# Retention values of two head pairs in products of 512 columns, weights passing four accumulating banks; keys, queries and the gated unit's operands by halves

## The chip, the cores and the metric

The kernel runs on one core of one Trainium2 chip. The metric is the time of one execution on the device in microseconds (us); less is better. A core has a matrix engine (TensorE, PE in the profile; its weight loads are listed as PEld), a vector engine (VectorE, DVE), an activation engine (ScalarE, ACT), a general engine (GpSimd, POOL), and a queue from which this kernel issues its DMA transfers (SyncE, SP). Each engine works through its own instructions in a fixed order and waits on the others by semaphores.

## The reference

Input and output are 1024 tokens of 1024 channels. There are two layers, each `x = x + mixer(rmsnorm(x))`, and a final rmsnorm. Layer 0 is one input projection that feeds a state-space branch with a gated unit and a retention branch, and an output projection over both. Layer 1 is a convolution module. The change lies in layer 0:

```python
def mixer_ab(h, w_in, ...):
    proj = h @ w_in
    u_s5, g_s5, q, k, v, g_ret = jnp.split(proj, cuts, axis=-1)
    y_s5 = s5_mixer(u_s5, ...)       # ends with y = gelu(y); y * sigmoid(y @ glu_w + glu_b)
    y_s5 = y_s5 * jax.nn.silu(g_s5)
    q, k: (B, L, 8 heads, 64);  v: (B, L, 8 heads, 128)
    y_ret = retention(q, k, v) * jax.nn.silu(g_ret)
    return jnp.concatenate([y_s5, y_ret], axis=-1) @ w_out

def retention(q, k, v):              # chunks of 64 frames
    q = rope(q, positions) * (RET_DK ** -0.5)
    k = rope(k, positions)
    scores = jnp.einsum('bnihd,bnjhd->bnhij', qc, kc) * intra
    intra_out = jnp.einsum('bnhij,bnjhe->bnihe', scores, vc)
    kv = jnp.einsum('bnjhd,jh,bnjhe->bnhde', kc, k_dec, vc)
    # s <- chunk_decay * s + kv, from chunk to chunk
    cross = jnp.einsum('bnihd,ih,bnhde->bnihe', qc, q_dec, s_prev)
    out = intra_out + cross
    return (out - mean) * rsqrt(var + EPS)      # per head
```

## The kernel before

**Products.** A product of two fp32 operands is made of three: each operand is split into a high part (a rounded copy, tile names with h) and a low part (what is left, names with l), and high x high, high x low and low x high are summed in one PSUM bank (`mm3`, L119; 128 contraction rows each, eight row blocks `KB`). Weights arrive as tiles of 128 x 1024 through `wnext` and `wload_pieces` (L87 to L117): a DMA of 512 KB into `wf`, a cast on ACT into `wh` (L115), a subtraction on POOL into `wl` (L116). Each of the three has three buffers, and loads run two tiles ahead of use, in the order that `plan` (L63) writes down. Activations `xs[h]` lie in SBUF, split, in two halves h of 512 tokens.

**Banks.** PSUM has three banks in `ps_mm` (`bank(..., aux=False)`) and five in `ps_aux` in this part of the program.

**Retention** (L766) works on four pairs of heads. `ret_proj(pair)` (L791) projects the keys, then the queries: two halves of 24 products with 512 columns each, the weights stationary, and an eviction on DVE that multiplies by the norm's factor (L804). `turn` (L807) does the rotary positions: four DMAs on SP copy `raw` into `swp` with its blocks of 32 partitions exchanged (L813, one swap buffer), POOL multiplies both by tables (L816, L817; four instructions of half the tokens each), and DVE adds the halves into `krot` or `qrot` (L818). The adds of the keys are held back behind the last query eviction (L824). Then come the values of the pair (L829 to L844): for each of eight token blocks 24 products of 256 columns, here with the tokens as the stationary operand and the weights as the moving one, in a bank of `ps_mm`, and an eviction on ACT (L844).

`y_pass` (L757) belongs to the other branch: it loads outputs of the state-space part, transposed, applies gelu on ACT and stores them on SP; from pair 1 on it is held behind the last statistics of the pair before.

`ret_heads(pair, K, Q, V)` (L847) takes the rotated tiles: eight transposes of the keys (`ktp`, L856), `kt` with the decay on DVE (L858), 28 products `kv` (L870), the states `S` by a chain of DVE instructions (L878, L880), the scores `sp` (L886) and their mask on DVE (`sc`, L892), the outputs `ro` (L912, L917), the per-head norm on DVE (L926, L927, L932, tiles `on` with three buffers), and transposes `rt` of the normalised tiles (L940), multiplied by the gate `grl` (L943) and stored (L946). The two halves of tokens are `0` and `1` in names such as `rt1`. The transposes of a pair come in the order first half head 1, head 0, then second half head 1, head 0, and `on` of the last tile takes a buffer that a transpose of the first half frees.

**Order of the work.** The scheduler of the language merges what is written one after the other: while the heads of one pair wait on DVE, the keys and queries of the next pair run on PE, and PE's order is fixed when the program is built. `chained` (L357) keeps groups of products together, and `issue_after` holds an instruction behind another.

**Changeover.** `layer0_back_and_layer1` (L953) begins with the gated unit. Its operands `y` are loaded by `load_split` (L963) as eight tiles of 128 x 1024 in the weights' `wf` buffers, each split into halves: `yh` on ACT (L950) and `yl` on DVE (L951). The loop at L991 then makes 16 groups of 24 products `mm_glu`. The scheduler runs the first of them beside the heads of pair 3. The table of the convolution, `convw`, is loaded and halved on DVE at L1082 to L1084.

Of the kernel before, what the change touches and what calls it, by code (L numbers as in the profile page):

```python
# [39 lines left out]
class Trunk:  # L40
# [22 lines left out]
    def plan(self):  # L63

        A = self.A
        seq = [(A["w_ab"][nb], f"u{nb}") for nb in range(8)]
        seq += [(A["w_ab"][nb], f"g{nb}") for nb in range(8, 24)]
        for p in range(4):
            seq += [(A["w_ab"][28 + p], f"k{p}"), (A["w_ab"][24 + p], f"q{p}")]
            seq += [(A["w_v"][2 * p + i], f"v{p}_{i}") for i in range(2)]  # L70
        seq += [(A["w_glu"][nb], f"glu{nb}") for nb in range(8)]

        def wo(h):
            return [q for nb in range(8) for q in ((A["w_out"][nb], f"wos{nb}_{h}"),
                                                   (A["w_out"][8 + nb], f"wor{nb}_{h}"))]
# [681 lines left out]
    def y_pass(self, rp, cb):  # L757
# [4 lines left out]
        yn = rp.tile([P, P, 8], F32, name=f"yn_{cb}", tag="ynt", bufs=2)  # L762
# [3 lines left out]
    def retention(self, st):  # L766
# [11 lines left out]
        nc.sync.dma_start(self.g128[:], A["ret_g128"])  # L778
        for pair in range(4):
            cur = self.ret_proj(pair)  # L780
# [8 lines left out]
            self.ret_heads(pair, *cur)  # L789

    def ret_proj(self, pair):  # L791
# [5 lines left out]
        def project(nm):  # L797
            w = self.wnext(f"{nm}{pair}")
            raw = raws[nm] = self.rq.tile([P, T], F32, name=f"{nm}raw_{pair}", tag="raw", bufs=2)
            for h in range(2):  # L800
                c = slice(h * HALF, (h + 1) * HALF)
                ps = self.bank(f"mm_{nm}{pair}_{h}", aux=False)
                self.gemm(ps[:], w, self.xs[h])
                last = nc.vector.tensor_tensor(raw[:, c], ps[:], self.R[:, c], op=ALU.mult)  # L804
# [16 lines left out]
        project("k")  # L821
        krot, adds = turn("k")
        last = project("q")
# [4 lines left out]
        for add in adds:  # L828
            add()  # L829

        wv = [self.wnext(f"v{pair}_{i}") for i in range(2)]
        vt = rp.tile([P, 8, 256], F32, name=f"v_{pair}", tag="v", bufs=2)
        for b in range(8):
            ps = self.bank(f"mm_v{pair}_{b}", aux=False)
            h, o = b // 4, (b % 4) * P
            for kb in range(KB):
                xh, xl = self.xs[h][kb]
                i, k4 = kb // 4, kb % 4
                wh = wv[i][0][:].rearrange("p (k a) n -> p k (a n)", a=2)[:, k4, :]
                wl = wv[i][1][:].rearrange("p (k a) n -> p k (a n)", a=2)[:, k4, :]  # L840
                nc.tensor.matmul(ps[:, :256], xh[:, o:o + P], wh, start=kb == 0, stop=False)  # L841
                nc.tensor.matmul(ps[:, :256], xh[:, o:o + P], wl, start=False, stop=False)  # L842
                nc.tensor.matmul(ps[:, :256], xl[:, o:o + P], wh, start=False, stop=kb == KB - 1)  # L843
            nc.scalar.mul(vt[:, b, :], ps[:, :256], self.Rtok[:, b:b + 1])  # L844
        return krot, qrot, vt

    def ret_heads(self, pair, K, Q, V):  # L847
        nc, rp = self.nc, self.rp
        v = nc.vector

# [11 lines left out]
        for hf in range(2):  # L862
            ps = self.bank(f"kv{hf}_{pair}")
            for b4 in range(4):
# [3 lines left out]
                for hh in range(2):  # L868
                    r = slice(64 * hh, 64 * hh + 64)
                    nc.tensor.matmul(ps[r, b4 * P:(b4 + 1) * P], kt[:, b, r], V[:, b, hh * P:(hh + 1) * P],  # L870
# [32 lines left out]
        for hf in range(2):  # L903
            pss = [self.bank(f"ro{hf}_{2 * pair + hh}") for hh in range(2)]

            def products():
# [7 lines left out]
                for hh in range(2):  # L914
                    for b4 in range(4):
                        b = 4 * hf + b4
                        yield nc.tensor.matmul(pss[hh][:, b4 * P:(b4 + 1) * P], sc[hh][:, b, :],  # L917
                                               V[:, b, hh * P:(hh + 1) * P], start=False, stop=b4 == 3)
# [34 lines left out]
    def layer0_back_and_layer1(self, st):  # L953
# [9 lines left out]
        def load_split(src, name, halves):  # L963
# [6 lines left out]
            if halves:  # L970
                for h in range(2):
                    for kb in range(KB):
# [18 lines left out]
        for nb, h in [(nb, h) for nb in range(6) for h in range(2)] + [(6, 0), (7, 0), (6, 1), (7, 1)]:  # L991
# [14 lines left out]
            v.scalar_tensor_tensor(b[:], sg[:], 0.5, a[:].bitcast(F32), op0=ALU.mult, op1=ALU.subtract)  # L1006
# [77 lines left out]
        v.tensor_scalar(cw[:], cw[:], 0.5, None, op0=ALU.mult)  # L1084
# [261 lines left out]
def layout(inp):  # L1346
# [10 lines left out]
    wv = w[:, 3072:4096].reshape(2, 4, P, 4, 256)  # L1357
# [50 lines left out]
```

## Time and profile before

| | us |
|---|---|
| median of 3 runs | 1220.06 (1220.02 to 1220.82) |
| the profiled execution | 1225.77 |
| its span, first to last instruction | 1224.0 |
| PE busy in it | 1203.9 |
| retention in the trace | about 337 to 556 |
| changeover to the gated unit | about 556 to 594 |

The mean granted clock of PE in the profiled execution is 0.995 of full speed. Busy times of PE are sums of the durations of overlapping products, cut where they overlap, so a busy PE can still be a PE at less than its best pace; the distance between the starts of two products is the measure of pace. Rows that begin with a line such as L841 are groups of instructions: line, engine, operation, tiles (output<-inputs), shape, count, then busy us and mean ns of one, then the idle time of the engine before them and what ended it. Rows that begin with two times are single instructions or short runs of them in order of time.

### The profile page before, as it was taken

The numbers are of one execution on the slowest core, as the hardware profiler recorded it, in microseconds if no ns is written. First come the engines' busy times: TensorE is split into PE (matmuls) and PEld (weight loads), VectorE is DVE, ScalarE is ACT, GpSimd is POOL, SyncE is SP. The second block draws the span as 40 slices with busy tenths as digits, with TensorE's granted clock in tenths as the row PEclk, the third lists the DMA queues.
The fourth block names the chain that finished last, engine by engine and source line by source line (L and its number), as shares of the span: only waits on it lengthen the run. The fifth ranks groups of instructions, "written<-read, shape, count | busy, mean of one in ns | idle before, by whom it ended". The sixth has DMA issues, their size and how long they took to land.

```text
span 1224.0 us, 17472 instructions
## 1 busy us (share of the span) xinstructions
PE 1203.9 (98%) x6676; PEld 1015.3 (83%) x6676; DVE 770.8 (63%) x1357; ACT 470.3 (38%) x698; POOL 719.6 (59%) x472
## 2 busy tenths in 40 slices
PE   9999999999999999998999999999999999999987
PEld 7888888888889999897888787888888887888877
DVE  7965555555414644646646102399999999899664
ACT  7212333232222323234435322554435474435653
POOL 2059988888124333352444553777795789769742
PEclk9999999999999999999999999999999999999998
DMA  9342433333384536376445654533445323345443
GB/s 330 104 138 75 151 126 126 137 123 123 115 258 138 171 106 185 92 215 220 164 155 182 213 167 119 153 103 93 132 147 192 101 69 112 109 124 172 155 147 138
DMA packets 86115, 179.93 MB, mean 147 GB/s; under 512 B 7696, under 2 KB 36624, under 8 KB 85392
## 3 DMA queue, kind: packets, MB, share of 16 engines
q1 hardware_dynamic: 86032, 178.82, 46.2%
q8 instruction: 52, 0.85, 0.3%
q14 instruction: 31, 0.25, 0.1%
HBM read 135.87 MB, written 38.73 MB: 143 GB/s over the span
## 4 chain that ended last, share of the span: by engine, by line
PE 89%; DMA 4%; DVE 2%; ACT 2%; issue 1%; POOL 1%; SPq 1%; DVEq 0%; POOLq 0%; ACTq 0%
PE mm_g L126 7%; PE mm_g L125 7%; PE mm_g L124 7%; PE mm_wo L126 4%; PE mm_wo L125 4%; PE mm_wo L124 4%; PE mm_a L126 2%; PE mm_b L126 2%; PE mm_b L125 2%; PE mm_b L124 2%; PE mm_a L125 2%; PE mm_a L124 2%; PE mm_u L126 2%; PE mm_u L125 2%; PE mm_u L124 2%; PE mm_glu L126 2%
## 5 line engine op out<-in xcount | busy, mean ns | idle before, releaser
L1114 DVE SCALAR_TENSOR_TENSOR cv<-u,convw,cv 128x512 f32<-128x512 f32 x416 | 283.6, 749 | 15.4 <-ACT cv L1106 13.8
L126 PE MATMUL mm_g<-xh,wl_g 128*128 128x512 f32 x256 | 100.8, 394 | 0.0
L125 PE MATMUL mm_g<-xl,wh_g 128*128 128x512 f32 x256 | 100.7, 393 | 0.0
L124 PE MATMUL mm_g<-xh,wh_g 128*128 128x512 f32 x256 | 100.5, 393 | 0.0
L841 PE MATMUL mm_v<-wh_v,xh 128*128 128x256 f32 x256 | 72.5, 283 | 0.6 <-ACT v L844 0.6
L843 PE MATMUL mm_v<-wh_v,xl 128*128 128x256 f32 x256 | 72.5, 283 | 0.0
L842 PE MATMUL mm_v<-wl_v,xh 128*128 128x256 f32 x256 | 72.4, 283 | 0.0
L116 POOL TENSOR_TENSOR wl_v<-wf_v,wh_v 128x1024 fp32r<-128x1024 f32 x8 | 19.6, 2449 | 87.7 <-ACT wh_v L115 87.7
L1102 POOL TENSOR_TENSOR tp<-tp,tp 128x512 f32<-128x512 f32 x48 | 62.2, 1297 | 6.7 <-ACT tp L1101 4.2
L307 DVE TENSOR_TENSOR gt<-mm_g,R 128x512 f32<-128x512 f32 x32 | 21.9, 684 | 59.9 <-PE mm_g L126 59.9
L126 PE MATMUL mm_oc<-zh,wl_woc 128*128 128x512 f32 (+1 forms) x152 | 54.3, 360 | 3.4 <-DVE wl_woc L116 3.4
L125 PEld LDWEIGHTS mm_g<-xl,wh_g 128*128 128x128 f32 x256 | 48.1, 188 | 11.3 <-issue 1.6
L116 POOL TENSOR_TENSOR wl_wos<-wf_wos,wh_wos 128x1024 fp32r<-128x1024 f32 x16 | 38.8, 2426 | 30.9 <-ACT wh_wos L115 30.9
L126 PEld LDWEIGHTS mm_g<-xh,wl_g 128*128 128x128 f32 x256 | 48.0, 188 | 10.6
L1026 DVE TENSOR_TENSOR x<-mm_wo,xr 128x512 f32<-128x512 f32 x16 | 11.1, 691 | 72.1 <-PE mm_wo L126 69.0
L124 PEld LDWEIGHTS mm_g<-xh,wh_g 128*128 128x128 f32 x256 | 48.1, 188 | 9.6
L124 PE MATMUL mm_oc<-zh,wh_woc 128*128 128x512 f32 (+1 forms) x152 | 55.8, 371 | 0.0
L116 POOL TENSOR_TENSOR wl_cb<-wf_cb,wh_cb 128x1024 fp32r<-128x1024 f32 x16 | 38.5, 2408 | 28.0 <-ACT wh_cb L115 23.1
L125 PE MATMUL mm_oc<-zl,wh_woc 128*128 128x512 f32 (+1 forms) x152 | 54.7, 361 | 0.0
L125 PE MATMUL mm_glu<-yl,wh_glu 128*128 128x512 f32 x128 | 50.3, 393 | 2.2 <-DVE yl L951 2.2
L116 POOL TENSOR_TENSOR wl_wor<-wf_wor,wh_wor 128x1024 fp32r<-128x1024 f32 x16 | 38.8, 2426 | 22.7 <-ACT wh_wor L115 22.7
L125 PE MATMUL mm_u<-xl,wh_u 128*128 128x512 f32 x128 | 50.1, 391 | 1.0 <-DVE xl L239 1.0
(384 smaller groups left out, 3728.4 us busy)
## 6 DMA issues: line engine op xcount, KB each, us to landing
wf_g<-w_ab SPq DMA_DIRECT2D x16, 512.0 KB, 4.4
wf_wos<-w_out SPq DMA_DIRECT2D x16, 512.0 KB, 3.7
wf_wor<-w_out SPq DMA_DIRECT2D x16, 512.0 KB, 3.7
wf_cb<-w_c SPq DMA_DIRECT2D x16, 512.0 KB, 3.6
wf_ca<-w_c SPq DMA_DIRECT2D x16, 512.0 KB, 3.7
wf_woc<-w_out_c SPq DMA_DIRECT2D x16, 512.0 KB, 4.0
wf_cg<-w_c SPq DMA_DIRECT2D x11, 512.0 KB, 3.7
u_d<-ut SPq DMA_DIRECT2D x8, 512.0 KB, 3.3
```

The lines of the kernel that those rows point to most:

```text
L116: lo[i].tensor_tensor(wl[:].rearrange(fl)[:, c], wf[:, c], h.bitcast(F32), op=ALU.subtract)
L124: nc.tensor.matmul(ps, wh[:, kb, :], xh, start=start, stop=False)
L125: nc.tensor.matmul(ps, wh[:, kb, :], xl, start=False, stop=False)
L126: self.last_mm = nc.tensor.matmul(ps, wl[:, kb, :], xh, start=False, stop=stop)
L307: nc.vector.tensor_tensor(gt[:, c], ps[:], self.R[:, c], op=ALU.mult)
L841: nc.tensor.matmul(ps[:, :256], xh[:, o:o + P], wh, start=kb == 0, stop=False)
L842: nc.tensor.matmul(ps[:, :256], xh[:, o:o + P], wl, start=False, stop=False)
L843: nc.tensor.matmul(ps[:, :256], xl[:, o:o + P], wh, start=False, stop=kb == KB - 1)
L1026: v.tensor_tensor(t[:], ps[:], xt[:], op=ALU.add)
L1102: gp.tensor_tensor(s0[:], s0[:], sk[:], op=ALU.add)
L1114: v.scalar_tensor_tensor(dst[:], us[i][:, k:k + HALF], cw[:, nb, k:k + 1], accs_[i][:], op0=ALU.mult, op1=ALU.add)
```

## The change

Four things are altered.

1. **Values.** `ret_values(pair)` replaces the values in `ret_proj` and is called for pairs 0 and 2 only. It makes the values of two pairs at once: for each half of the tokens four banks of `ps_aux` are opened, four weight tiles pass, and each weight tile gives every bank 2 x 3 products of 512 columns. A half ends with four evictions of 128 x 512. Each weight tile is loaded once per half, 16 loads of values in all where there were 8. The weights are laid out anew on the host for it.
2. **Order of keys and queries.** `ret_proj` is a generator that stops after the key products. Pair 2's keys are projected ahead of the heads of pair 1; the values of pairs 2 and 3 then come between the heads of pair 1 and those of pair 2. Pair 3's halves come in the order key, query, key, query. There are two swap buffers for one, and one `ynt` buffer for two.
3. **Operands of the gated unit.** `load_split` loads them by halves of the tokens, first all of the first half; a `wf` buffer holds two of them.
4. **The convolution's table** is halved behind the last instruction of the gated unit.

```diff
@@ plan
-            seq += [(A["w_v"][2 * p + i], f"v{p}_{i}") for i in range(2)]
+            if p % 2 == 0:
+                seq += [(A["w_v"][2 * p + j], f"v{p}_{h}_{j}") for h in range(2) for j in range(4)]
@@ y_pass
-        yn = rp.tile([P, P, 8], F32, name=f"yn_{cb}", tag="ynt", bufs=2)
+        yn = rp.tile([P, P, 8], F32, name=f"yn_{cb}", tag="ynt", bufs=1)
@@ retention
+        ahead = None
         for pair in range(4):
-            cur = self.ret_proj(pair)
+            proj = ahead or self.ret_proj(pair)
+            K, Q = list(proj)[-1]
+
+            ahead = pair == 1 and self.ret_proj(pair + 1)
+            if ahead:
+                next(ahead)
+            if pair % 2 == 0:
+                V = self.ret_values(pair)
...
-            self.ret_heads(pair, *cur)
+            self.ret_heads(pair, K, Q, V)
@@ ret_proj
             for h in range(2):
-                c = slice(h * HALF, (h + 1) * HALF)
-                ps = self.bank(f"mm_{nm}{pair}_{h}", aux=False)
-                self.gemm(ps[:], w, self.xs[h])
-                last = nc.vector.tensor_tensor(raw[:, c], ps[:], self.R[:, c], op=ALU.mult)
-            return last
+                yield half(nm, w, raw, h)
...
-            swp = self.rq.tile([P, T], F32, name=f"{nm}swp_{pair}", tag="swp", bufs=1)
+            swp = self.rq.tile([P, T], F32, name=f"{nm}swp_{pair}", tag="swp", bufs=2)
...
-        project("k")
+        k, q = project("k"), project("q")
+
+        for step in ((k, q, k) if pair == 3 else (k, k)):
+            next(step)
+        yield None
         krot, adds = turn("k")
-        last = project("q")
+        for last in q:
+            pass
...
-        wv = [self.wnext(f"v{pair}_{i}") for i in range(2)]
-        vt = rp.tile([P, 8, 256], F32, name=f"v_{pair}", tag="v", bufs=2)
-        for b in range(8):
-            ps = self.bank(f"mm_v{pair}_{b}", aux=False)
...
-                nc.tensor.matmul(ps[:, :256], xh[:, o:o + P], wh, start=kb == 0, stop=False)
-                nc.tensor.matmul(ps[:, :256], xh[:, o:o + P], wl, start=False, stop=False)
-                nc.tensor.matmul(ps[:, :256], xl[:, o:o + P], wh, start=False, stop=kb == KB - 1)
-            nc.scalar.mul(vt[:, b, :], ps[:, :256], self.Rtok[:, b:b + 1])
-        return krot, qrot, vt
+        yield krot, qrot
+
+    def ret_values(self, pair):
+
+        nc = self.nc
+        res = []
+        for h in range(2):
+            vt = self.rp.tile([P, 4, HALF], F32, name=f"v_{pair}_{h}", tag="v", bufs=2)
+            pss = [self.bank(f"mm_v{pair}_{h}_{b}") for b in range(4)]
+            for j in range(4):
+                wh, wl = (t[:].rearrange("p (k a) n -> p k (a n)", a=4) for t in self.wnext(f"v{pair}_{h}_{j}"))
+                for b in range(4):
+                    o = slice(b * P, (b + 1) * P)
+                    for k in range(2):
+                        kb = 2 * j + k
+                        xh, xl = self.xs[h][kb]
+                        nc.tensor.matmul(pss[b][:], xh[:, o], wh[:, k, :], start=kb == 0, stop=False)
+                        nc.tensor.matmul(pss[b][:], xh[:, o], wl[:, k, :], start=False, stop=False)
+                        nc.tensor.matmul(pss[b][:], xl[:, o], wh[:, k, :], start=False, stop=kb == KB - 1)
+            for b in range(4):
+                nc.scalar.mul(vt[:, b, :], pss[b][:], self.Rtok[:, 4 * h + b:4 * h + b + 1])
+            res.append(vt)
+        return res
@@ load_split
-            if halves:
-                for h in range(2):
-                    for kb in range(KB):
-                        f = lp.tile([P, HALF], F32, name=f"{name}f{kb}_{h}", tag="tp", bufs=3)
-                        nc.sync.dma_start(f[:], src[rows(kb), hs(h)])
-                        put(kb, h, f[:])
-            else:
+            for h in range(2):
                 for kb in range(KB):
-                    f = self.wp.tile([P, T], F32, name=f"{name}f{kb}", tag="wf", bufs=3)
-                    nc.sync.dma_start(f[:], src[rows(kb)])
-                    for h in range(2):
-                        put(kb, h, f[:, hs(h)])
+                    if halves:
+                        f = lp.tile([P, HALF], F32, name=f"{name}f{kb}_{h}", tag="tp", bufs=3)[:]
+                        nc.sync.dma_start(f, src[rows(kb), hs(h)])
+                    else:
+
+                        if kb % 2 == 0:
+                            f2 = self.wp.tile([P, 2, HALF], F32, name=f"{name}f{kb}_{h}", tag="wf", bufs=3)
+                        f = f2[:, kb % 2, :]
+                        nc.sync.dma_start(f, src[rows(kb), hs(h)])
+                    put(kb, h, f)
@@ gated unit, convolution
-            v.scalar_tensor_tensor(b[:], sg[:], 0.5, a[:].bitcast(F32), op0=ALU.mult, op1=ALU.subtract)
+            glu_end = v.scalar_tensor_tensor(b[:], sg[:], 0.5, a[:].bitcast(F32), op0=ALU.mult, op1=ALU.subtract)
...
-        v.tensor_scalar(cw[:], cw[:], 0.5, None, op0=ALU.mult)
+        with self.tc.issue_after(glu_end.ins):
+            v.tensor_scalar(cw[:], cw[:], 0.5, None, op0=ALU.mult)
```

In the built program after the change, PE's order between pair 1's last query product and the values of pair 2 is: 48 key products of pair 2, 8 transposes `ktp` of pair 1, 22 query products of pair 2, `kv` of pair 1, scores with 9 query products among them, `ro` of pair 1, the last 17 query products of pair 2, then the 16 transposes `rt` of pair 1 with nothing between them. On DVE, both halves of pair 1's `qrot` and one key eviction of pair 2 come before pair 1's `kt`, and the last normalised tile of pair 1 comes behind pair 2's last query eviction, both halves of its `krot` and two gate products. On SP, pair 1's query swap copies stand behind one gate load for two before.

More of the change, by code (lines that the diff above doesn't have):

```diff
@@ L800, in project, with half @@
             for h in range(2):
-                c = slice(h * HALF, (h + 1) * HALF)
-                ps = self.bank(f"mm_{nm}{pair}_{h}", aux=False)
-                self.gemm(ps[:], w, self.xs[h])
-                last = nc.vector.tensor_tensor(raw[:, c], ps[:], self.R[:, c], op=ALU.mult)
-            return last
+                yield half(nm, w, raw, h)
+        def half(nm, w, raw, h):
+            c = slice(h * HALF, (h + 1) * HALF)
+            ps = self.bank(f"mm_{nm}{pair}_{h}", aux=False)
+            self.gemm(ps[:], w, self.xs[h])
+            return nc.vector.tensor_tensor(raw[:, c], ps[:], self.R[:, c], op=ALU.mult)
         def turn(nm, behind=None):
             raw, tab = raws[nm], tabs[nm]
-            swp = self.rq.tile([P, T], F32, name=f"{nm}swp_{pair}", tag="swp", bufs=1)
+            swp = self.rq.tile([P, T], F32, name=f"{nm}swp_{pair}", tag="swp", bufs=2)
             o = rp.tile([P, T], F32, name=f"{nm}rot_{pair}", tag=f"{nm}rot", bufs=1)
@@ L849, in ret_heads @@
         v = nc.vector
+        val = lambda b, hh: V[b // 4][:, b % 4, (2 * (pair % 2) + hh) * P:(2 * (pair % 2) + hh + 1) * P]
         kt = rp.tile([P, 8, P], F32, name=f"kt_{pair}", tag="kt", bufs=1)
@@ L869, in ret_heads @@
                     r = slice(64 * hh, 64 * hh + 64)
-                    nc.tensor.matmul(ps[r, b4 * P:(b4 + 1) * P], kt[:, b, r], V[:, b, hh * P:(hh + 1) * P],
+                    nc.tensor.matmul(ps[r, b4 * P:(b4 + 1) * P], kt[:, b, r], val(b, hh),
                                      start=True, stop=True)
@@ L917, in products @@
                         yield nc.tensor.matmul(pss[hh][:, b4 * P:(b4 + 1) * P], sc[hh][:, b, :],
-                                               V[:, b, hh * P:(hh + 1) * P], start=False, stop=b4 == 3)
+                                               val(b, hh), start=False, stop=b4 == 3)
             last_ro = self.chained(products())
@@ L1356, in layout @@
     A["w_ab"] = _blocks(order)
-    wv = w[:, 3072:4096].reshape(2, 4, P, 4, 256)
+    wv = w[:, 3072:4096].reshape(4, 2, P, 2, HALF)
     A["w_v"] = wv.transpose(3, 0, 2, 1, 4).reshape(8, P, KB, P)
```

6 lines of the change are left out of this document (removed).

## The prediction

> **What bounds the kernel now.** I read the shares first, then the chain of waits, then a table of stretches, then single instructions.
>
> ```profile
> span 1224.0 us, 17472 instructions
> PE 1203.9 (98%) x6676; PEld 1015.3 (83%) x6676; DVE 770.8 (63%) x1357; ACT 470.3 (38%) x698; POOL 719.6 (59%) x472
> PE 89%; DMA 4%; DVE 2%; ACT 2%; issue 1%; POOL 1%; SPq 1%; DVEq 0%; POOLq 0%; ACTq 0%
> 337.00:556.00 219.00, 218.44 (x1593) 198.53 (x1590) 100.08 (x241) 61.46 (x79) 80.67 (x49) 1.00 0.55 166
> ```
>
> The last row is the retention stage: length, then PE, PEld, DVE, ACT and POOL busy (instructions), granted clock, DMA share, GB/s. Rows of the timeline further down begin with start and duration in us; a bracket gives the idle time before and what ended it. PE has 0.56 us free in 219 us. So only two things count: how long PE needs for its products, and which new wait reaches it. Outside this stage and the changeover to the gated unit (556 to about 594 us) the order of every engine's instructions stays as it is.
>
> **Term 1: the value products.** 768 products of 256 columns become 384 of 512. They overlap in the pipeline, so the price is the distance between two starts, not the duration.
>
> ```profile
> L841 PE MATMUL mm_v<-wh_v,xh 128*128 128x256 f32 x256 | 72.5, 283 | 0.6 <-ACT v L844 0.6
> ...
> 533.11 0.28 PE L841 MATMUL mm_v<-wh_v,xh 128*128 128x256 f32 x1
> ...
> 556.02 0.28 PE L843 MATMUL mm_v<-wh_v,xl 128*128 128x256 f32 x1
> ...
> 356.84 0.39 PE L125 MATMUL mm_q<-xl,wh_q 128*128 128x512 f32 x1
> ...
> 359.10 0.39 PE L126 MATMUL mm_q<-xh,wl_q 128*128 128x512 f32 x1
> ```
>
> Pair 3's 192 value products start over 533.11 to 556.02: 22.91/191 = 0.120 us each. The query products of 512 columns take (359.10-356.84)/10 = 0.226; elsewhere, just after transposes, up to 0.230. I take 0.228: 768 x 0.120 - 384 x 0.228 = 92.2 - 87.6 = -4.6 us (-5.4 to -3.9). A reader of the durations 0.283 and 0.39 would expect -67; that is the trap of this change.
>
> The only PE gap in the stage goes too. It came when an eviction stood behind a gelu on ACT:
>
> ```profile
> 368.68 0.39 PE L841 MATMUL mm_v<-wh_v,xh 128*128 128x256 f32 x1 [0.56 <-ACT v L844]
> ```
>
> Now the next half's first bank is finished 18 products (4.1 us) before it is wanted again, which covers a delay of this size: -0.6 (0 if the gelu falls later in the four). The evictions themselves, 16 wide ones for 32, lie beside PE and count nothing.
>
> **Term 2: weights of pair 0's values.** Each weight tile is now loaded once per half: 16 subtractions on POOL for 8, and a tile lasts 24 x 0.228 = 5.5 us on PE. Query products end at 359.33, so the fourth tile's low part is wanted near 359.33 + 3 x 5.5 + 0.2 = 376.0.
>
> ```profile
> 367.78 2.38 POOL L116 TENSOR_TENSOR wl_k<-wf_k,wh_k 128x1024 fp32r<-128x1024 f32 x1
> ...
> 434.34 1.29 POOL L816 TENSOR_TENSOR qraw<-qraw,ropeq 128x512 f32<-128x512 f32 x1 [10.03 <-DMA qswp<-qraw]
> ...
> 438.09 1.75 POOL L817 TENSOR_TENSOR qswp<-qswp,ropeq 128x512 f32<-128x512 f32 x1
> ```
>
> POOL ends the key's rotation where its next row starts, 367.8. Its new order from there is: third tile 2.4, four query operations 434.34 to 439.84 = 5.5, fourth tile 2.4, so 378.1: late by 2.1. The second swap buffer lets the query rotation come that early. Eight more weight loads of 512 KB and eight more casts on ACT pass engines that are 0.55 and 0.28 busy in this stage: nothing. I take +1.7 (0 if the query's copies land after the fourth tile's weights are ready; 2.5).
>
> **Term 3: pair 1's keys wait for the query rotation.** Until now the 192 value products stood between the last query product (417.80, call it E) and the transposes of the keys:
>
> ```profile
> 417.80 0.28 PE L841 MATMUL mm_v<-wh_v,xh 128*128 128x256 f32 x1
> ...
> 440.84 1.04 PE L856 MATMUL ktp<-ident,krot 128*128 128x128 f32 x8
> ...
> 446.63 1.75 PE L870 MATMUL kv<-v,kt 128*64 128x128 f32 x28
> ```
>
> Afterwards pair 1 has no value products. PE's order after E is 48 key products of pair 2, 8 transposes, 22 query products of pair 2, then kv: 48 x 0.228 + 0.8 + 22 x 0.228 = E + 16.8. kv needs kt, and in DVE's new order kt stands behind qrot of pair 1 and one key eviction. So I follow qrot:
>
> ```profile
> 416.83 1.57 SPq L946 DMA_DIRECT2D yr_d<-grl  x2
> 423.32 1.59 SPq L900 DMA_DIRECT2D grl<-gr_d  x2
> 425.00 2.44 SPq L813 DMA_DIRECT2D qswp<-qraw  x4
> ...
> DMA to landing us min/median/max: 2.3/5.6/7.7
> ...
> 439.87 0.69 DVE L818 TENSOR_TENSOR qrot<-qraw,qswp 128x512 f32<-128x512 f32 x1 [1.19 <-POOL qswp L817]
> 441.47 1.29 DVE L858 TENSOR_TENSOR kt<-ktp,kdec 128x512 f32<-128x512 f32 x2 [0.92 <-PE ktp L856]
> ...
> 498.99 2.87 DVE L818 TENSOR_TENSOR qrot<-qraw,qswp 128x512 f32<-128x512 f32 x1 [1.18 <-POOL qswp L817]
> ```
>
> On SP the swap copies still stand behind a gate load that waits for a store (423.32); only the second gate load now follows them. So they go out at 424.1, the last near 425.9 (E + 8.1). Landing 5.6: E + 13.7. POOL 5.5: E + 19.2. The second qrot half takes 0.69 alone, or 2.87 where POOL goes straight on to a weight tile, as at 498.99; here one is waiting, but half of the difference may overlap: 1.8. Eviction 0.7 and half of kt 0.65: E + 22.3, against E + 16.8: **+5.5**. Low end: landing 2.3 and qrot 0.69, +1.1. High end: landing 7.5 (what 434.34 was) and 2.87, +8.5. What is late next: S, the score products and pair 2's query eviction behind them, all of which keep their distances.
>
> **Term 4: no products between pair 1's transposes.** R is the end of the pair's last ro products. The same place one pair later, before:
>
> ```profile
> 515.83 0.61 PE L917 MATMUL ro<-v,sc 128*128 128x128 f32 x4
> ...
> 522.44 1.03 PE L940 MATMUL rt<-ident,on 128*128 128x128 f32 x8
> ...
> 519.92 1.37 DVE L932 TENSOR_SCALAR on<-ro,mv,rs 128x128 f32<-128x128 f32 x4
> 521.29 0.66 DVE L804 TENSOR_TENSOR kraw<-mm_k,R 128x512 f32<-128x512 f32 x1
> 523.08 1.37 DVE L932 TENSOR_SCALAR on<-ro,mv,rs 128x128 f32<-128x128 f32 x4 [1.13 <-PE rt L940]
> 524.36 1.28 DVE L943 TENSOR_TENSOR grl<-rt,grl 128x512 f32<-128x512 f32 x2
> ```
>
> R is about 516.3. Before, PE ran 27 products until the first transposes and 24 more before the second, which come later than the DVE rows shown. Afterwards it has 17 products (3.9) and rt0 (0.8), done R + 4.7, then rt1 at once, then pair 2's values. rt1 needs the third normalised tile, whose buffer rt0 frees and which on DVE stands behind: the tile before (done 521.2 = R + 4.9), an eviction 0.7, both krot halves of pair 2 (1.4 alone), two gate products 1.3, itself 1.3: R + 9.6. So PE stands **+4.8** (4.2 if ends overlap; 7.8 if POOL slows krot to 1.8 and 2.9). I take krot's own input as in time: its copies begin near E + 22, and before krot is wanted come all of kv, scores, ro and their statistics; were it late, the high end holds some of that.
>
> **Term 5: the clock after a stall.** Two PE gaps of before are over 2 us:
>
> ```profile
> 560.98 0.50 PE L125 MATMUL mm_glu<-yl,wh_glu 128*128 128x512 f32 x1 [2.16 <-DVE yl L951]
> ...
> 562.00:563.00 1.00, 1.00 (x4) 0.63 0.82 242
> 563.00:565.00 2.00, 2.00 (x19) 0.50 1.06 389
> 565.00:567.00 2.00, 2.00 (x30) 0.83 0.69 274
> ...
> 1169.33 0.50 PE L126 MATMUL mm_oc<-zh,wl_woc 128*128 128x512 f32 x1 [3.44 <-DVE wl_woc L116]
> ...
> 1170.00:1175.00 5.00, 5.00 (x16) 0.68 0.80 262
> ```
>
> (Columns here: length, PE busy, clock, DMA, GB/s.) After 2.16 us of idling the clock falls short by 0.37 + 2 x 0.5 + 2 x 0.17 = 1.7 us of work; after 3.44 by 5 x 0.32 = 1.6. To shorter gaps I give none. So terms 3 and 4 each bring **+1.5** more (0 if under 2 us, to 1.7). *The Trainium skill, "TensorE: Matmul & The Clock Gate", Part 1, states that the clock halves after an idle window of about 3.4 us and recovers after 3.4 busy ones. The dip after 3.44 us agrees; that after 2.16 us is earlier than the page says, and the trace decides. By the page alone each stall would cost an estimated 1.7 us, and a wait of 2 to 3 us nothing.*
>
> **Term 6: the changeover.** Two gaps and that dip lie here.
>
> ```profile
> 560.04 0.29 DVE L1084 TENSOR_SCALAR convw<-convw 128x248 f32<-128x248 f32 x1 [6.15 <-DMA convw<-conv_w]
> ...
> 576.56 1.76 PE L912 MATMUL ro<-S,qrot 64*128 64x128 f32 x16 [1.03 <-DVE S L880]
> ```
>
> DVE stood 6.15 us for a table of the convolution, and yl behind it: 2.16 + 1.7 + 1.03 = 4.9 us lost. The table's scaling moves behind the gated unit, and the y operands come in halves beside pair 3. New there: pair 3's krot closes on its transposes. From the last key product PE has 24 query products, 8 transposes and 27 gated products = 51 x 0.228 + 0.8 = 12.4 us; krot needs eviction 0.7, copies 1.8 + 5.6 (the last issue, its landing), POOL's first half 2.7, DVE 1.8 = 12.6: +0.2. With that, a gap like the 1.03 for S, and as much again for the query's rotation behind it, I set 2.0 lost: **-2.9** (-4.9 to 0).
>
> **Sum.** -4.6 - 0.6 + 1.7 + 5.5 + 4.8 + 2 x 1.5 - 2.9 = +6.9. The profiled execution (span 1224.0) would show about 1231; its run lies above the median of the runs, 1220.06, and I move that by the same amount: **1227.0 us**.
>
> **Rivals.**
> - *The copies come early*: pair 1's swap lands 2.3 us after issue, term 3 is +1.1 and too short for a dip: 1227.0 - 4.4 - 1.5 = 1221.1, not slower by 0.2%. It decides if the copies are in by E + 10.5 (428.3). For: the minimum of that row. Against: in pair 1 itself they took 7.5 behind two gate loads.
> - *Neither wait is there*: kt and the third tile are ready because DVE's chains are shorter than I add them. -4.6 - 0.6 + 1.7 - 2.9 = -6.4: 1213.7. For: PE never waited in pairs 1 and 2 of before. Against: DVE's order is fixed and its durations are rows.
> - *The chains run later*: both high ends, +3.0 and +3.0: 1233.0. For: more weight tiles on POOL, beside which a rotation took 2.87.
> - *Bank changes cost*: 64 changes of bank in 384 products. The nearest rows:
>
> ```profile
> 529.56 0.49 PE L124 MATMUL mm_q<-xh,wh_q 128*128 128x512 f32 x1
> 529.89 0.40 PE L125 MATMUL mm_q<-xl,wh_q 128*128 128x512 f32 x1
> ...
> 532.88 0.39 PE L126 MATMUL mm_q<-xh,wl_q 128*128 128x512 f32 x1
> ```
>
> The step out of transposes, 0.33, is 0.10 longer than a common one: 64 x 0.10 = +6.4, 1233.4. Against: 532.88 to 533.11, a change of bank, is an ordinary 0.23. *The same page's section "A second HAM failure mode: psum-queue depth-cycling" reports products that cycle through banks losing the clock to small idles; before changes bank every 24 products at clock 1.00, so the trace does not bear it out yet.*
>
> **Chances.** Forecast 0.43, with its own range 1223 to 1231; early copies 0.20; no waits 0.22; later chains 0.10; bank changes 0.05. About 0.2% (2.4 us) can be told from no change. Faster: 0.22 + 0.03 of early copies + 0.02 of the forecast's tail = 0.27. Same: 0.13 + 0.03 = 0.16. Slower: 0.57. The range goes from just under the case without waits to the later chains: 1213 to 1233.
>
> **What would show it.** 384 value products at 0.228 us and no gap at a change of bank (term 1); one gap of about 2 us at a low weight part of pair 0 (2); a gap of 5 to 6 us at kv of pair 1, ended by kt (3); a gap near 5 us at rt1 of pair 1, ended by the normalised tile (4); a granted clock near 0.5 for some 3 us behind both (5); no DVE wait for the table, PE gaps under 2 us at the transposes of pair 3 (6). PE without gaps at kv and rt1 would make the forecast wrong.

## The result, and the profile after

| | us |
|---|---|
| before, median of 6 runs | 1220.35 (1218.86 to 1220.95) |
| after, median of 6 runs | 1230.3 (1227.73 to 1234.24) |
| ratio | 1.0083, 95% interval 1.0071 to 1.0095 |
| forecast | 1227.0 (1213 to 1233) |
| profiled execution before / after | 1225.77 / 1231.35, spans 1224.0 / 1229.3 |

The change makes the kernel 9.95 us slower; 6.9 were forecast. Its runs also scatter more than those of before; why was not followed up. First the page of the changed kernel, then the table of stretches (length, PE, PEld, DVE, ACT, POOL busy, granted clock, DMA share, GB/s), then the table of PE's waits (waited for, total us, times, longest):

```profile
span 1229.3 us, 16778 instructions
PE 1202.6 (98%) x6292; PEld 998.3 (81%) x6292; DVE 764.7 (62%) x1357; ACT 475.6 (39%) x690; POOL 738.9 (60%) x480
```

```profile
337.00:560.00 223.00, 213.69 (x1184) 178.42 (x1181) 91.89 (x238) 65.98 (x73) 86.65 (x47) 0.97 0.50 159
453.00:510.00 57.00, 47.70 (x275) 40.16 (x274) 30.17 (x78) 14.24 (x16) 24.82 (x16) 0.88 0.55 176
```

```profile
PE kv L894 <- DVE kt L882: 4.8, 1, 4.8
PE rt L964 <- DVE on L956: 4.5, 1, 4.5
PE ktp L880 <- DVE krot L829: 2.1, 1, 2.1
...
PE sp L910 <- DVE qrot L829: 0.8, 1, 0.8
...
PE mm_glu L126 <- DVE yl L975: 0.6, 1, 0.6
```

Busy shares hardly tell that 10 us were lost; the table of stretches does. Where PE had 0.56 us free in 219, it now has 9.3 in 223, all of it in the heads of pair 1, and the clock there is 0.88. The table of waits then names both gaps and their releasers, as the prediction had them.

Now the two gaps on the timeline, with the instructions that lead up to them. E, the end of pair 1's query products, is 437.55 here.

```profile
442.46 0.32 SPq L924 DMA_DIRECT2D grl<-gr_d  x1
442.88 2.43 SPq L824 DMA_DIRECT2D qswp<-qraw  x4
...
449.77 1.30 POOL L827 TENSOR_TENSOR qraw<-qraw,ropeq 128x512 f32<-128x512 f32 x1 [5.71 <-DMA qswp<-qraw]
...
455.27 2.81 DVE L829 TENSOR_TENSOR qrot<-qraw,qswp 128x512 f32<-128x512 f32 x1 [1.17 <-POOL qswp L828]
458.01 0.68 DVE L816 TENSOR_TENSOR kraw<-mm_k,R 128x512 f32<-128x512 f32 x1
458.61 1.27 DVE L882 TENSOR_TENSOR kt<-ktp,kdec 128x512 f32<-128x512 f32 x2
459.34 0.91 PE L894 MATMUL kv<-v,kt 128*64 128x128 f32 x6 [4.83 <-DVE kt L882]
...
477.03 1.37 DVE L956 TENSOR_SCALAR on<-ro,mv,rs 128x128 f32<-128x128 f32 x4
...
478.40 0.66 DVE L816 TENSOR_TENSOR qraw<-mm_q,R 128x512 f32<-128x512 f32 x1
478.97 1.28 DVE L829 TENSOR_TENSOR krot<-kraw,kswp 128x512 f32<-128x512 f32 x2
480.18 1.28 DVE L967 TENSOR_TENSOR grl<-rt,grl 128x512 f32<-128x512 f32 x2
481.37 1.36 DVE L956 TENSOR_SCALAR on<-ro,mv,rs 128x128 f32<-128x128 f32 x4
482.79 1.97 PE L964 MATMUL rt<-ident,on 128*128 128x128 f32 x8 [4.48 <-DVE on L956]
```

Read backwards from each bracket: kv waits for kt, kt for a key eviction, that for the second qrot half (2.81 beside a weight tile on POOL), that for POOL, that for the copies, which landed 6.9 us after their first issue and stood on SP behind a gate load. At rt the chain is DVE alone: five groups of instructions one after the other from 477.03 on, with no wait between them.

The granted clock behind the first gap (length, PE busy, clock, DMA, GB/s):

```profile
459.00:461.00 2.00, 1.66 (x16) 0.50 0.78 207
461.00:462.00 1.00, 1.00 (x14) 0.50 0.90 201
462.00:463.00 1.00, 1.00 (x10) 0.50 0.95 160
463.00:464.00 1.00, 1.00 (x16) 0.62 0.82 311
```

At 0.50 the value products behind the second gap start 0.43 us apart (485.41 to 486.69 in three steps), against 0.227 at 1.00, so a busy microsecond there does about half the work; the sums here take it as half and are some 6% high by that. From 459.34 to 464 the loss is 0.83 + 0.5 + 0.5 + 0.38 = 2.2 us; the same sum behind the second gap is 2.4, behind the one at 572.49 (573 to 580) 3.1.

**The account.** In these two executions the first product of the output projection starts at 661.7 and at 671.4, and pair 0's keys at 337.45 and 337.22: 9.9 us more lie between. The parts: value products -5.0 (below), the gap behind the eviction -0.6, first gap 4.83 + 2.2, second 4.48 + 2.4, changeover 2.05 + 0.55 + 0.79 + 3.1 against 4.9 before, +1.6. Sum +9.9. After that the two executions differ in work that the change does not touch: before's has the gap of 3.44 us and its dip near its end (of the other runs only run 7 shows that gap), which is most of the reason why its span lies only 5.3 us below. The medians, 9.95 apart, agree with the account.

### The profile page after: what moved, and what is told of

Same layout as the page of the kernel before. It is cut to its first block, busy times and chain, and to the rows that moved or that the text cites. A ratio compares the mean times of both kernels' runs of the same rounds, so it can differ in the third digit from the quotient of the medians.

```text
span 1229.3 us, 16778 instructions
## 1 busy us (share of the span) xinstructions
PE 1202.6 (98%) x6292; PEld 998.3 (81%) x6292; DVE 764.7 (62%) x1357; ACT 475.6 (39%) x690; POOL 738.9 (60%) x480
## 4 chain that ended last, share of the span: by engine, by line
PE 89%; DMA 3%; DVE 2%; POOL 2%; ACT 2%; issue 1%; SPq 1%; DVEq 0%; POOLq 0%; ACTq 0%
PE mm_g L127 7%; PE mm_g L126 7%; PE mm_g L125 7%; PE mm_wo L127 5%; PE mm_wo L126 5%; PE mm_wo L125 5%; PE mm_v L863 2%; PE mm_v L862 2%; PE mm_v L864 2%; PE mm_a L127 2%; PE mm_b L127 2%; PE mm_b L126 2%; PE mm_b L125 2%; PE mm_a L126 2%; PE mm_a L125 2%; PE mm_u L127 2%
## 5 line engine op out<-in xcount | busy, mean ns | idle before, releaser
L117 POOL TENSOR_TENSOR wl_v<-wf_v,wh_v 128x1024 fp32r<-128x1024 f32 x16 | 38.5, 2414 | 53.3 <-ACT wh_v L116 53.3
L125 PE MATMUL mm_glu<-yh,wh_glu 128*128 128x512 f32 x128 | 51.1, 401 | 0.0
L127 PE MATMUL mm_glu<-yh,wl_glu 128*128 128x512 f32 x128 | 50.9, 398 | 0.0
L127 PE MATMUL mm_b<-h1h,wl_cb 128*128 128x512 f32 x128 | 50.6, 395 | 0.0
```

Of the source, the lines that this page charges most:

```text
L117: lo[i].tensor_tensor(wl[:].rearrange(fl)[:, c], wf[:, c], h.bitcast(F32), op=ALU.subtract)
L125: nc.tensor.matmul(ps, wh[:, kb, :], xh, start=start, stop=False)
L127: self.last_mm = nc.tensor.matmul(ps, wl[:, kb, :], xh, start=False, stop=stop)
```

## The experiments

The kernel before that ran beside each of them, on the same chip, took 1220.6 to 1222.4 us, so ratios are compared rather than times. Gaps and clocks are read from one execution of each kernel. The diffs are excerpts, with `...` where lines are left out.

**1. The query's copies first.** In the changed kernel, pair 1's gate loads stand behind the query copies on SP:

```diff
...
-            nc.sync.dma_start(gt[:], self.gr_d[h * P:(h + 1) * P])
+            with ExitStack() as held:
+                if pair == 1:
+                    held.enter_context(self.tc.issue_after(self.swap["q"].ins))
+                nc.sync.dma_start(gt[:], self.gr_d[h * P:(h + 1) * P])
```

> The changed kernel, but both gate loads of pair 1 stand behind the query's four swap copies on SP. Theory (the wait of 4.83 us at pair 1's kv is the query rotation, late because its copies stand behind a gate load): the copies go out at about E + 1 instead of E + 5.3, the wait falls from 4.83 us to under 1 us, the dip of the granted clock behind it (2.2 us) goes with it, and the time falls by 5 to 7 us from 1230.3 to about 1224. Rival (POOL and DVE work sets kt, or the copies only land later in a busier DMA): wait and dip stay within 1 us, time stays near 1230.

Measured: 1224.39 us, ratio 1.0035 (1.0021 to 1.0049). PE's gap in its timeline, and the copies that lead to it:

```profile
438.94 4.06 SPq L825 DMA_DIRECT2D qswp<-qraw  x4
...
446.88 1.29 POOL L828 TENSOR_TENSOR qraw<-qraw,ropeq 128x512 f32<-128x512 f32 x1 [2.71 <-DMA qswp<-qraw]
...
456.50 2.11 PE L895 MATMUL kv<-v,kt 128*64 128x128 f32 x28 [2.08 <-DVE kt L883]
```

The time fell as the theory said, 1.0083 to 1.0035. The wait fell by 2.75 us, not by the 4 expected: with E at 437.45 the copies went out at E + 1.5 instead of E + 5.3, but landed at E + 9.4 instead of E + 12.2. A gap of 2.08 us still has its dip (1.7 us). The gap at kv scatters: in runs 2 to 4, which leave everything ahead of it alone, it is 4.8, 3.4 and 4.0 us, so the gate load ahead of the copies is worth 1.3 to 2.75 us, about half of the gap; the rest is the length of the rotation itself. That the median fell by more than this trace shows (its execution, 1228.63 us, is the slowest of the eight) is not explained.

**2. The last normalised tile first.** On DVE that tile of pair 1 goes ahead of two gate products, the query eviction and krot:

```diff
...
+                    with ExitStack() as held:
+                        if pair == 1 and hb == 0:
+                            held.enter_context(self.tc.issue_after(self.last_on.ins))
+                        v.tensor_tensor(gts[hh][:, c], tp[:], gts[hh][:, c], op=ALU.mult)
...
+            with ExitStack() as held:
+                if pair == 2 and nm == "q" and h:
+                    held.enter_context(self.tc.issue_after(self.last_on.ins))
+                return nc.vector.tensor_tensor(raw[:, c], ps[:], self.R[:, c], op=ALU.mult)
```

> The changed kernel, but on DVE the last normalised tile of pair 1 goes ahead of two gate products, a query eviction and both halves of pair 2's krot. Theory (the wait at pair 1's second transposes is the sum of these DVE instructions): the wait of 4.48 us falls by about 3.1 to about 1.4 us, too short for a dip of the clock (2.4 us), so the time falls by about 5.5 us to about 1225. Rival (the dip comes after any stall here): the wait falls by 3.1, the dip stays, time about 1227. Second rival (the norm itself is late): wait stays over 4 us.

Measured: 1231.76 us, ratio 1.0084 (1.0056 to 1.0113): nothing won. Its PE gaps:

```profile
480.66 1.09 PE L967 MATMUL rt<-ident,on 128*128 128x128 f32 x8 [1.70 <-DVE on L959]
...
501.64 0.50 PE L866 MATMUL mm_v<-wl_v,xh 128*128 128x512 f32 x1 [2.39 <-POOL wl_v L117]
```

At the place itself the theory holds: 4.48 became 1.70, and the clock behind it stays 1.00. The gain was given back downstream, and the larger part by the edit itself. Pair 2's values begin 2.9 us earlier (481.51 for 484.41). But the edit also holds back the query eviction on DVE (481.72 for 478.40), so the query rotation reaches POOL 4.6 us later (493.80 for 489.21), and the fourth weight tile, which stands behind it there, is now 2.39 us late, with a dip behind it (0.50 from 503 to 505). In this execution the changeover's gap, 3.21 us, is longer too. A wait that goes can reappear at the next thing that it had covered.

**3. Useless products in the gap.** 19 products of 512 columns between the two groups of transposes; their result is read by nobody:

```diff
+                if hb and pair == 1:
+                    dm, xh = self.bank("fill"), self.xs[0][0][0]
+                    last_ro = self.chained((nc.tensor.matmul(dm[:], xh[:, :P], xh[:], start=i == 0, stop=i == 18)
+                                            for i in range(19)), last_ro)
```

> The changed kernel with 19 products of 512 columns whose result nobody reads, put on PE between the first and the second transposes of pair 1 (4.3 us of the wait of 4.48 us). Theory (idling of PE lowers the clock behind it): the wait shrinks to under 0.5 us, clock behind it stays at 1.00, and the time falls by the dip alone, about 2.4 us, to about 1228, though PE has more to do. Rival (the low clock there comes from something else): clock still near 0.5 for some 4 us behind the transposes, time unchanged at 1230.

Measured: 1228.18 us, ratio 1.0059 (1.0034 to 1.0084). A stretch of 2 us behind the transposes:

```profile
482.00:484.00 2.00, 2.00 (x10) 1.00 1.11 295
```

PE no longer waits at rt, the clock is 1.00 where it was 0.50, and the time falls by 2.1 us of medians, 2.9 by ratios; 2.4 were expected. Intervals of this width overlap with the changed kernel's own, and other gaps moved in this execution (3.4 us at kv, 3.7 at pair 3's scores), so the clock is the verdict here: idling of PE lowers it, and products whose result nobody reads were enough to keep it.

**4. Pair 3's key copies first.** The operand loads from the seventh row block on stand behind them:

```diff
...
+                        with ExitStack() as held:
+                            if h or kb >= 6:
+                                held.enter_context(self.tc.issue_after(self.swap["k"].ins))
+                            nc.sync.dma_start(f, src[rows(kb), hs(h)])
```

> The changed kernel, but the loads of the y operands from the seventh row block on stand behind pair 3's key swap copies on SP. Theory (term 6 failed because these copies stood behind operand loads that waited for a store of gelu's result): copies go out about 2 us earlier (near 558.7 instead of 560.7), the wait of 2.05 us at pair 3's first key transposes goes to about 0, the dip of 3.1 us behind it goes too, time falls by 4 to 5 us to about 1226. Rival (the operands are then late instead): a wait of 1 to 3 us at a gated product, ended by yl, with the dip still there; time within 1.5 us of 1230.

Measured: 1231.44 us, ratio 1.0094 (1.0069 to 1.0118).

```profile
569.39 0.73 PE L125 MATMUL mm_glu<-yh,wh_glu 128*128 128x512 f32 x2 [0.90 <-ACT yh L975]
...
583.01 1.16 PE L911 MATMUL sp<-qrot,krot 64*128 64x128 f32 x16 [1.76 <-DVE qrot L830]
```

The copies go out at 556.65, as soon as their source is written (556.62), and the wait at the key transposes is gone, as the theory said. The time has not fallen. The operands came late, as the rival said, and the query rotation became the next wait, with a dip behind it (0.64 and 0.51 in the two stretches after 584).

**5. The table alone.** The kernel before, with only the halving of the convolution's table moved behind the gated unit (the last hunk of the diff).

> The kernel before with one edit only: the halving of the convolution's table stands behind the gated unit. Theory: this removes the wait of 2.16 us at the second gated product and the dip of 1.7 us behind it, so 1220.4 becomes about 1216.5. Rival (the operands wait for their own loads there anyway): a wait of 1 to 2 us ended by yh or yl stays, and the time stays within 1.5 us of 1220.4.

Measured: 1218.77 us, ratio 0.9977 (0.9964 to 0.999), about -2.8 us. Its gaps at the changeover are 0.17, 0.52 and 1.12 us, and the clock stays at 1.00; the two larger ones:

```profile
566.13 0.50 PE L125 MATMUL mm_glu<-yl,wh_glu 128*128 128x512 f32 x1 [0.52 <-DVE yl L951]
573.56 1.75 PE L912 MATMUL ro<-S,qrot 64*128 64x128 f32 x16 [1.12 <-DVE S L880]
```

This part of the change is a gain by itself, of about the size that term 6 gave it (2.16 + 1.7, less small waits behind): from pair 0's keys to the output projection the two traces take 320.9 us for 324.2.

**6. The values spread.** The changed kernel, but the second group of values is made half by half, at the places where before the values of pairs 1 and 2 stood; pair 2's keys are no longer ahead:

```diff
...
-            ahead = pair == 1 and self.ret_proj(pair + 1)
-            if ahead:
-                next(ahead)
-            if pair % 2 == 0:
-                V = self.ret_values(pair)
+            for h in ((0, 1), (0,), (1,), ())[pair]:
+                self.ret_values(2 * (pair > 0), h)
+            V = self.vt[pair]
...
```

> The changed kernel, but the second group of values is made by halves of the tokens: the first half between pair 1's queries and its heads, the second between pair 2's queries and its heads, 96 products of 512 columns (21.8 us) at each place; pair 2's keys are not projected ahead; evictions go to tiles of 256 columns. Theory (both waits of pair 1 come from the missing products, not from the wide products): no PE wait over 1 us in pairs 1 and 2, so the 4.83 + 2.2 + 4.48 + 2.4 = 13.9 us go and 1230.3 becomes about 1216. Rival (the wide products or their weights cost time by themselves): waits gone, but more than 1219, with PE gaps at value products.

Measured: 1227.52 us, ratio 1.0045 (1.0032 to 1.0058). PE's two gaps in pairs 1 and 2, and POOL before the first:

```profile
456.35 0.50 PE L862 MATMUL mm_v<-wl_v,xh 128*128 128x512 f32 x1 [2.44 <-POOL wl_v L116]
...
517.49 0.50 PE L862 MATMUL mm_v<-wl_v,xh 128*128 128x512 f32 x1 [2.86 <-POOL wl_v L116]
...
442.89 1.06 ACT L115 CAST wh_v<-wf_v 128x1024 fp32r<-128x1024 f32 x1 [4.61 <-PE mm_v L863]
...
448.52 1.29 POOL L826 TENSOR_TENSOR qraw<-qraw,ropeq 128x512 f32<-128x512 f32 x1 [5.55 <-DMA qswp<-qraw]
...
453.96 2.34 POOL L116 TENSOR_TENSOR wl_v<-wf_v,wh_v 128x1024 fp32r<-128x1024 f32 x1
```

With products back in those places the waits at kv and at rt are gone: they did come from the missing products. In their place PE waits for the fourth weight tile, so the time is not the 1216 of the theory but over 1219, with gaps at value products, as the rival had it. The rival's reason, that the wide products cost time by themselves, does not follow from that: the cast of the tile was done at 443.9, and POOL then stood 5.55 us for the query's copies, with the subtraction queued behind the rotation. Run 9 tests this.

**7. Spread, with whole operands.** The kernel before with the values of run 6 and the moved table, but operands in whole tiles, pair 3's keys before its queries, and one swap buffer, as before.

> The kernel before with the wide value products spread as in the run beside it, and the table's halving moved; operands of the gated unit in whole tiles, pair 3's keys before its queries, one swap buffer, as before. Against that run it undoes the halves of the operands and of pair 3. Theory (these halves help a changeover that has no value products to cover it): the changeover loses 3 to 8 us more here than in the run beside it, time about 1220. Rival (they do nothing): same time within 1.5 us.

Measured: 1243.93 us, ratio 1.0178 (1.016 to 1.0197). The gaps at the fourth weight tile grow:

```profile
461.62 0.79 PE L851 MATMUL mm_v<-wl_v,xh 128*128 128x512 f32 x1 [6.55 <-POOL wl_v L116]
```

and 5.99 us in pair 2. From the last value product to the last gated product it is 677.4 - 531.4 = 146.0 us, against 664.9 - 522.2 = 142.7 in run 6: in these two executions the halves and the order of pair 3 are worth 3.3 us at the changeover, inside the theory's range. The time is far from the 1220 that it gave: most of the 16 us between the two runs lies in pairs 1 and 2, where the run differs from run 6 by one swap buffer for two and by the place where the pieces are written. The traces show the way it goes: pair 1's query copies go out at 444.88, behind both gate loads and just as krot's second half, which reads the only swap buffer, ends (444.85), where run 6 has them out at 441.71 behind one gate load; and they land 9.0 us after the first issue, for 6.8. How much each of the two edits takes was not tried.

**8. Spread, with pair 3's key copies first** (the edits of 6 and 4 together).

> The spread version with pair 3's key copies ahead of the operand loads on SP, as in the fourth run. There the wait only moved from the key transposes to the scores (2.1 us) with a later dip. Theory: the same here, time within 2 us of the spread version, about 1216. Rival (with pair 1 free of waits the copies gain): 3 to 5 us under the spread version, about 1212.

Measured: 1229.63 us, ratio 1.0055 (1.0034 to 1.0075). As the theory had it: the key transposes wait no more, the scores wait 1.40 and 1.77 us, nothing is won (the 2.1 us over run 6 lie within the intervals).

**9. Spread, with POOL's order mended.** On POOL the query rotation of pairs 1 and 2 goes behind the fourth weight tile, and the program writes the rotation behind the values:

```diff
...
+            with ExitStack() as held:
+                if nm == "q" and pair in (1, 2):
+                    held.enter_context(self.tc.issue_after(self.wl_ins[f"v2_{pair - 1}_3"].ins))
+                for c in cs:
+                    nc.gpsimd.tensor_tensor(raw[:, c], raw[:, c], tab[:, 0, c], op=ALU.mult)
...
```

> The spread version, but on POOL the four operations of the query rotation in pairs 1 and 2 stand behind the subtraction of the fourth value weight tile, and the rotation is written behind the values. Theory (the waits of 2.44 and 2.86 us at value products in the spread version come from POOL's order alone: it sat idle 5.55 us for the copies with this subtraction ready behind them): both waits go to under 0.5 us with the dip behind the first (1.7 us), time 5 to 7 us under the spread version, that is about 1 us under the kernel before of the same call. Rival (the subtraction waits for its load or cast): waits stay over 1.5 us, time as in the spread version, about 5 us over the kernel before.

Measured: 1219.88 us against 1222.43 for the kernel before beside it, ratio 0.9986 (0.9974 to 0.9998). Its stretches (length, PE busy, clock, DMA, GB/s) and its one gap over 1 us between 337 and 600:

```profile
337.00:450.00 113.00, 113.00 (x586) 1.00 0.59 185
450.00:555.00 105.00, 105.00 (x639) 1.00 0.52 166
```

```profile
559.13 1.12 PE L884 MATMUL ktp<-ident,krot 128*128 128x128 f32 x4 [3.21 <-DVE krot L831]
```

PE is never idle from 337 to 555 us, at full clock: the waits are gone and the time came out about as the theory had it, and the rival is out. The wide products with their weights cost nothing beyond their pace; what was slow in retention was where they stood. The changeover still loses its 3.21 us and a dip (0.50 from 560 to 565).

**10. The same, with both of pair 3's copies ahead of later operand loads on SP.**

> The run beside it, and on SP pair 3's key copies ahead of the operand loads from the seventh row block on, its query copies ahead of the second half's loads from the third row block on. Theory (the changeover loses some 6 us because both rotations of pair 3 stand in SP's queue behind operand loads): PE waits at the key transposes and the scores of pair 3 sum to under 2 us, no dip there, time 4 to 6 us under the run beside it. Rival (the chain of one rotation is longer than the gated products that cover it, whatever the queue): the waits still sum to 3 us or more, at the scores or at an operand of the second half, time within 2 us of the run beside it.

Measured: 1218.5 us, ratio 0.9973 (0.9957 to 0.9989). The gap at the key transposes is gone, the scores and the operands wait in its place, 3.3 us in all; the two longest:

```profile
557.38 0.73 PE L124 MATMUL mm_glu<-yh,wh_glu 128*128 128x512 f32 x2 [0.65 <-ACT yh L978]
...
570.50 1.64 PE L914 MATMUL sp<-qrot,krot 64*128 64x128 f32 x16 [1.54 <-DVE qrot L831]
```

The gain over run 9 (1.4 us of medians) is within the intervals; the rival is nearer: in both orders of SP that were tried, one rotation is longer than what covers it in pair 3. Runs 9 and 10 and run 5 are faster than both kernels, but than the kernel before by only 0.1 to 0.3%, with intervals that end just under 1; run 5 and run 10 lie together at 0.9977 and 0.9973, and which of the two is faster is not settled.

## Why the prediction was right, and where it was not

- **Term 1, right.** Expected 0.228 us a product. Pair 2's and 3's run from 488.06 to 499.40 in 50 steps:

```profile
488.06 0.39 PE L862 MATMUL mm_v<-wh_v,xh 128*128 128x512 f32 x1
...
499.40 0.39 PE L864 MATMUL mm_v<-wh_v,xl 128*128 128x512 f32 x1
```

  11.34 / 50 = 0.227, 384 of them 87.1 us: -5.0 for -4.6. The bank changes, every six products here, do not show: the rival that priced them is out, and run 9 has no gap in all its value products.
- **Term 2, wrong: nothing for +1.7.** The wait has two ends, and both were off:

```profile
365.78 2.40 POOL L117 TENSOR_TENSOR wl_v<-wf_v,wh_v 128x1024 fp32r<-128x1024 f32 x1
...
374.04 7.56 POOL L117 TENSOR_TENSOR wl_v<-wf_v,wh_v 128x1024 fp32r<-128x1024 f32 x3
...
375.41 1.07 PE L862 MATMUL mm_v<-wh_v,xh 128*128 128x512 f32 x4
376.48 0.50 PE L863 MATMUL mm_v<-wl_v,xh 128*128 128x512 f32 x1
```

  POOL came to the third tile at 365.78, not at 367.8, and ended the fourth, the first of the three at 374.04, near 376.5, not at 378.1. And PE did not need it at its second product: the built order puts the four high x high products of that tile, one for each bank, first, 1.07 us of cover. I took the order of the source for the order of PE, without reading the built order there as I had for terms 3 and 4. That step hides the 0.8 us by which the tile was still late; had POOL come at 378.1, some 1.6 us of wait would have shown in spite of it. Run 10 shows 0.18 us at this place.
- **Term 3, right: 4.83 for 5.5.** The copies landed E + 12.2 for E + 13.7, qrot took 2.81 for 1.8. Run 1 shows SP's order as about half of it, run 6 that the missing products are its cause.
- **Term 4, right: 4.48 for 4.8**, instruction by instruction; run 2 takes 2.8 us of it away by DVE's order alone.
- **Term 5, right in kind, too small.** 2.2 and 2.4 us for 1.5 each: the clock stayed at 0.50 for about 4.4 and 4.8 us, where I looked for some 3. I had measured the dip behind the two gaps of before at 1.6 and 1.7, and taken less.
- **Term 6, wrong in sign: +1.6 for -2.9.** The table's part held (run 5). What failed is the step "krot +0.2": the gap is 2.05, with a dip of 3.1 us behind it that I had not given it, since I put it under 2 us. My chain began with the key eviction; on the chip SP was not free for the copies then:

```profile
557.98 0.69 DVE L816 TENSOR_TENSOR kraw<-mm_k,R 128x512 f32<-128x512 f32 x1 [0.47 <-PE mm_k L127]
...
559.37 1.27 SPq L1004 DMA_DIRECT2D yf<-yn_d  x3
560.69 2.42 SPq L824 DMA_DIRECT2D kswp<-kraw  x4
```

  The copies were ready at 558.7 and went out at 560.69, behind three operand loads, which the change issues by halves beside pair 3: the 2.0 us of the gap. I had named this queue for pair 1 and not looked at it for pair 3. The size is that of one execution: the waits at pair 3's key transposes and scores sum to 2.8 us there, and to 4.6, 3.2 and 4.6 in runs 1 to 3, which leave the changeover alone. Runs 4, 8 and 10 show that mending the queue alone wins nothing or little, since the query's rotation is next.

The miss of 3 us is thus term 6 (4.5 more) and term 5 (1.6 more), less term 2 (1.7), term 3 and term 4 (1.0 together) and term 1 (0.4). The two waits of pair 1 and their dips, 13.9 us measured for 13.3, are the mechanism that was forecast. That the whole came as near as 3 us is in part luck: terms 2 and 6 were both wrong, in opposite directions.

## What to carry to other kernels

A wide product that takes over the work of several narrow ones also takes away the places where those stood; before counting its pace, ask which wait each place covered, and give each its share back (run 9). Price a wait of the matrix engine with the clock behind it: here a gap of 2 to 5 us mostly cost 1.6 to 3 us more. And read the built order of every queue that the chain passes, the DMA queue first, at every place where the chain occurs.

## What the hardware showed that was not expected

The dip of the clock does not follow the length of the gap alone. Gaps of 2.05, 2.08, 2.16 and 2.44 us had one, and so had those of 1.76 and 1.54 in runs 4 and 10, close behind other idling; that of 1.70 in run 2 had none, and neither had the one of 2.86 us in run 6. In run 8 the gap at that same place, 2.84 us, had one: the clock there is 0.50 from 519 to 521. Run 6 first, then run 8:

```profile
517.00:519.00 2.00, 1.51 (x7) 1.00 0.99 418
519.00:521.00 2.00, 2.00 (x10) 1.00 0.73 293
```

```profile
517.54 0.50 PE L862 MATMUL mm_v<-wl_v,xh 128*128 128x512 f32 x1 [2.84 <-POOL wl_v L116]
```

Two gaps of one length at one place of almost the same program thus differ by a whole dip; what decides it is not in the rows.

The Trainium skill, "TensorE: Matmul & The Clock Gate", section "What's actually happening", says that the clock is set by a free-running window of about 3.4 us. That would fit with two equal gaps of which one falls across two windows, but no run here shows the windows; where they lay was not measured. The rule of the Trainium skill on that page (section "Why this matters for your kernels"), to allow no gaps of PE over about 3 us, was not strict enough here: gaps of 2.05 to 2.44 us had a dip.
